# Layer 0's triangular inverses: one DMA for each matrix stack and each result, GpSimd in program order

## The chip, the cores and the metric

The kernel runs on one core of a Trainium2 chip. The metric is the device time of one execution in microseconds, median of several runs; inputs and weights lie in HBM at the start, all outputs in HBM at the end.

## The reference

One inference step of a two-layer streaming encoder: 512 prompt tokens and 32 sample tokens with a stored state, model width 1024, all in float32. Layer 0 is RWKV-7 time mixing with 24 heads of 64, layer 1 differential attention; both add a memory cross-attention of four heads and a SiLU gate, and a final RMSNorm ends the trunk. What matters here is layer 0's recurrence, which the reference writes as a scan over tokens:

```python
def step(S, inp):
    r_t, k_t, v_t, w_t, kk_t, a_t = inp
    sa = jnp.einsum('bhvk,bhk->bhv', S, -kk_t)
    S = (S * w_t[:, :, None, :] + sa[..., None] * (kk_t * a_t)[:, :, None, :]
         + v_t[..., None] * k_t[:, :, None, :])
    return S, jnp.einsum('bhvk,bhk->bhv', S, r_t)
```

## The kernel before, in words

Tokens lie along the free dimension and features on the partitions. The 24 heads are worked on two at a time: 12 pairs of heads, numbered 0 to 11, each 128 columns wide. The scan is done in chunks of 64 tokens. Within a chunk, the effect of the tokens on each other is a unit triangular matrix that has to be inverted; the kernel inverts its 32 x 32 diagonal blocks and merges two blocks into one of 64 afterwards. A pair has 34 such blocks (32 of the prompt, 2 of the sample).

The life of one pair p, by the functions that follow:

- `rw_prep` makes the decayed keys and queries, and with matmuls the chunk matrices `at` (and `ats` for the sample). It is a generator of 33 parts. Part 24 makes the product `rkk` (on GpSimd for pairs 3 to 11, on VectorE for pairs 0 to 2), part 26 writes the 34 blocks to a DRAM tile `sc1` (`sc<-at`, `sc<-ats` in the profile), and part 27 has the matmul `ps_q` that reads `rkk`. Part 2 starts the `up` loads of the next pair.
- `rw_invert` loads the blocks back, one block per partition (`m<-sc`; for pair 1 the tile is a borrowed gate buffer, `sg<-sc`), and inverts all at once on GpSimd: a copy of the identity (`u<-ui`), then 31 steps of a multiply (`tm<-u,m`, L861) and an add (`u<-u,tm`, L863). To use more partitions, the 32 rows of an inverse are dealt to NCL = 3 partitions, so every block is loaded three times: 102 partitions. The 32 prompt blocks stand on partitions 0 to 95 and the two sample blocks on 96 to 101; six DMAs load them (three of 32 rows and three of 2 rows, each row 4 KB).
- `rw_back` writes the results to DRAM (`sc<-u`), also with six DMAs, in pieces of 128 B.
- `rw_at` reads them from there into `at` and `ats` (`at<-sc`, `ats<-sc`, five DMAs).
- `rw_merge` merges the blocks; it begins with VectorE transposes `t1b<-at`, which TensorE's `ps_w` reads.
- `rw_values`, `rw_chain`, `rw_sample`, `rw_outputs`, `rw_finish` run the recurrence over the chunks, store the states (`out<-so`) and normalise (`ps_y`, `yt`).

Layer 0's loop is a hand-made software pipeline. A stage is the chain of one pair, 23 steps long (`go("chain", pr)`). The list PLAN says, for each of the 23 steps and each of its two halves, which parts of the other pairs are emitted there: `("inv", 2, 0, 0)` at entry 12, second half, means that the inverse of pair pr + 2 is emitted there (below: entry 12.5). The last two numbers are estimated times by which `next(main)` spreads the projection matmuls (`ps_g`) between the entries; zeros leave that spread alone. Before stage 0, the lists FILL0 to FILL3 do the same for the first pairs. `rsq` emits the reciprocal square roots on VectorE for the next pair's norms ("the roots").

The order is fixed on four queues: `Queue` ties each instruction of TensorE, VectorE, ScalarE and of SyncE, which issues nearly all DMAs, to the one emitted before it. So SyncE's DMA queue (SPq) issues strictly in the order of emission, and a DMA that waits holds up those behind it. GpSimd isn't tied: its instructions are called on `nc.gpsimd` and placed by the scheduler.

The constant `ui`, the identity dealt to the 102 partitions, is made from a column `cls` that holds the class 0, 1 or 2 of a partition; with the order above it takes nine small VectorE operations.

Of the kernel before, what the change touches and what calls it, by code (L numbers as in the profile page):

```python
# [9 lines left out]
F32 = mybir.dt.float32  # L10
# [4 lines left out]
ALU = mybir.AluOpType  # L15
# [40 lines left out]
    [[("prep", 2, 0, 1.1), ("smp", 0, 0.21, 0.29)], [("prep", 2, 0, 0.86)]],  # L56
    [[("prep", 2, 1.1, 1.37)], []],
    [[("smp", 0, 0.21, 0)], [("prep", 2, 0, 0.9)]],
    [[("prep", 2, 1.1, 1.37)], [("back", 1, 0, 0)]],
    [[("smp", 0, 0.6, 0.85)], []],  # L60
    [[("prep", 2, 0.5, 0.58)], [("at", 1, 0, 0), ("fin", -1, 0, 1.0)]],
    [[("prep", 2, 0.36, 0.43)], [("inv", 2, 0, 0), ("fin", -1, 0, 0.84)]],
    [[("prep", 2, 0.36, 0.43)], [("fin", -1, 0, 0), ("prep", 3, 0, 0)]],
    [[("prep", 2, 0.25, 0)], [("fin", -1, 0, 0.98)]],
    [[("prep", 2, 0.4, 0), ("smp", 0, 0.11, 0)], [("prep", 3, 0, 0.6)]],
    [[("prep", 3, 0.53, 0)], [("mrg", 1, 0, 0.86)]],
    [[("prep", 3, 0.11, 0.17), ("mrg", 1, 0.9, 0)], [("rsq", 0, 0, 1.5)]],
    [[("prep", 3, 0.33, 0)], [("fin", -1, 0, 0.88)]],
    [[("prep", 3, 0.33, 0)], [("prep", 3, 0, 0.1), ("fin", -1, 0.6, 1.0)]],
# [4 lines left out]
SHIFTED, KEPT = 13, 24  # L74
LAM = 5
EARLY = 5
SPLIT = {10: (18,), 11: (1, 5, 9, 13)}
MPLAN = {10: [(0, 0), (2, 0), (3, 0), (4, 0), (5, 0), (6, 0), (6.5, 1), (7, 0), (8, 0), (9, 0), (10, 0), (11, 0), (11.5, 0), (12.5, 1),
# [12 lines left out]
NCL = 3  # L91
NBLK = 34
# [16 lines left out]
class Trunk:  # L109
# [77 lines left out]
    def consts_rwkv(self, c):  # L187

        nc, a = self.nc, self.a
# [40 lines left out]
        cl = c.tile([NCL * NBLK, 1], F32, name="cl")  # L230
        nc.gpsimd.iota(cl[:], pattern=[[0, 1]], base=0, channel_multiplier=1, allow_small_or_imprecise_dtypes=True)
        cls = c.tile([NCL * NBLK, 1], F32, name="cls")
        self.ve.tensor_scalar(cls[:], cl[:], 32.0, None, ALU.is_ge)
        for at, w in ((64, 1.0), (96, -2.0), (98, 1.0), (100, 1.0)):
            cl2 = c.tile([NCL * NBLK, 1], F32, name=f"cl{at}")
            self.ve.tensor_scalar(cl2[:], cl[:], float(at), None, ALU.is_ge)
            self.ve.scalar_tensor_tensor(cls[:], cl2[:], w, cls[:], ALU.mult, ALU.add)
        nc.gpsimd.iota(ii[:], pattern=[[NCL, nr], [-1, 32]], base=0, channel_multiplier=0,
                       allow_small_or_imprecise_dtypes=True)
        self.ve.tensor_scalar(self.ui[:], ii[:], cls[:, 0:1], 0.0, ALU.add, ALU.is_equal)  # L240
# [398 lines left out]
    def rw_prep(self, st, rkv):  # L639
# [108 lines left out]
        decayed(zr, 1, nk, de, 0)  # L748
        yield
        k2 = k  # L750
        spare = nc.gpsimd if pr > 2 else self.ve
        self.ve.tensor_tensor(k2[:], k[:], kf[:], ALU.mult)
        yield
        ba = p.tile([P, T], F32, tag="ta", name="ba", bufs=1)
# [85 lines left out]

    def rw_invert(self, st):

        nc, p, sc1 = self.nc, self.rb, st["sc1"]
# [12 lines left out]
        tm = p.tile([NCL * NBLK, self.nr, 32], F32, tag="tm", name="tm", bufs=1)  # L856
        for kx in range(31):
            n = kx // NCL + 1
            wd = 31 - kx
            sh = [NCL * NBLK, n, wd]  # L860
            nc.gpsimd.tensor_tensor(tm[:, :n, :wd], u3[:, :n, kx : kx + 1].to_broadcast(sh),  # L861
                                    m3[:, kx : kx + 1, kx + 1 :].to_broadcast(sh), ALU.mult)
            nc.gpsimd.tensor_tensor(u3[:, :n, kx + 1 :], u3[:, :n, kx + 1 :], tm[:, :n, :wd], ALU.add)  # L863

    def rw_back(self, st):

        u3 = st["u3"]
        st["sc2"] = [self.dp.tile([m, 32, 32], F32, tag=f"sc2{m}", name=f"sc2{m}", bufs=2) for m in (32, 2)]
        for o, t in zip((0, 96), st["sc2"]):
            m = t.shape[0]  # L870
            for q in range(NCL):
                n = len(range(q, 32, NCL))
                self.se.dma_start(t[:, q : 32 : NCL, :], u3[o + q * m : o + q * m + m, :n, :])

    def rw_at(self, st):

        at, ats, sc2 = st["at"], st["ats"], st["sc2"]
# [556 lines left out]
    def layer0(self, mem):  # L1434
# [6 lines left out]
        with ExitStack() as ctx:  # L1441
# [16 lines left out]
            for q in (1, 0, 2):  # L1458
# [1 line left out]
            sts = [{"pr": pr} for pr in range(NPAIR)]  # L1460
            run, mit = {}, {}
            make = {"fin": self.rw_finish, "val": self.rw_values, "mrg": self.rw_merge, "smp": self.rw_sample,
                    "out": self.rw_outputs, "chain": self.rw_chain}

            def go(kind, pr):

                if kind == "rsq":
                    self.rsqrt(self.r20[:], self.q20[:], self.rk0, "nt")
                elif 0 <= pr < NPAIR:
                    if kind in ("inv", "back", "at"):  # L1470
                        {"inv": self.rw_invert, "back": self.rw_back, "at": self.rw_at}[kind](sts[pr])
# [92 lines left out]
            def fill(n, each=6):  # L1564

                while n > 0:
                    for _ in range(min(n, each)):
                        next(main)
                    n -= each
                    self.some(LATER)  # L1570

            self.ordered = True
            for k, n in enumerate(FILL0):
                go("prep", 0)
                if k == 3:
# [18 lines left out]
            for k, n in enumerate(FILL2):  # L1594
                go("prep", 2)
                if k == 3:
                    go("rsq", 2)
                    go("inv", 1)
                    go("back", 0)
                    go("at", 0)  # L1600
                fill(n)
# [562 lines left out]
    def run(self):  # L2164
# [72 lines left out]
```

## Time and profile before

| | |
|---|---|
| median of 3 runs | 1403.37 us (1402.63 to 1403.77) |
| the profiled execution | 1402.28 us, span 1400.5 us |
| TensorE (PE) busy | 1361.5 us, 97% |
| VectorE (DVE) busy | 934.6 us, 67% |
| ScalarE (ACT) busy | 828.6 us, 59% |
| GpSimd (POOL) busy | 371.7 us, 27% |
| mean granted TensorE clock | 0.996 |

The span is the profiler's account of the execution from its first to its last instruction; the execution's own time has 1.8 us around it. Layer 0 takes the first half, up to about 700 us. In a row of a timeline stand the start and the duration in us, the engine, the line, the operation, the tiles as out<-in, the shape, the count of merged instructions, and in brackets the idle time before and what ended it. Most instructions carry L106, the line of the helper that records them, so they are told apart by their tiles. A row of waits reads: who waited for whom, us in total, times, longest. A row of a window reads: the stretch, its length, then the busy time and count of PE, PEld (weight loads), DVE, ACT and POOL, then the granted clock, the share of the 16 DMA engines and GB/s (where the row is of one engine alone, only that engine's time stands there).

### The profile page before, as it was taken

How to read it: one execution, taken by the hardware profiler on the slowest of the kernel's cores; microseconds unless marked ns; L12 is line 12 of the kernel's file. 1: busy time of each engine (PE TensorE's matmuls, PEld its weight loads, DVE VectorE, ACT ScalarE, POOL GpSimd, SP SyncE). 2: the span in 40 equal slices, each digit the busy share in tenths (PEclk: the TensorE clock that was granted, in tenths of full speed). 3: DMA queues.
4: the chain of work that ended last, by engine and by line, in shares of the span. 5: the costliest groups of instructions: out<-in, count | busy, mean ns of one | idle time of the engine just before them, and what ended most of it. 6: DMA issues, size and time to landing. Idle time of an engine off the chain costs nothing.

```text
span 1400.5 us, 31939 instructions
## 1 busy us (share of the span) xinstructions
PE 1361.5 (97%) x11893; PEld 1296.7 (93%) x11893; DVE 934.6 (67%) x2345; ACT 828.6 (59%) x2304; POOL 371.7 (27%) x841
## 2 busy tenths in 40 slices
PE   8999999999999999999999999999999999999997
PEld 6988899999998998897899999999999999999997
DVE  5765777787877787676753476676467756767443
ACT  5756677767776777565543366664466546665222
POOL 2136567555865576520000040000000001001000
PEclk9999999999999999999999999999999999999999
DMA  7543222332233222342474473333333322332321
GB/s 224 155 118 80 49 57 76 84 96 62 67 82 99 61 77 73 87 131 64 121 206 118 120 218 108 92 92 93 101 92 94 104 73 84 97 106 84 91 76 72
DMA packets 264036, 139.45 MB, mean 100 GB/s; under 512 B 57721, under 2 KB 252802, under 8 KB 263882
## 3 DMA queue, kind: packets, MB, share of 16 engines
q1 hardware_dynamic: 263818, 137.41, 34.9%
q8 instruction: 94, 1.54, 0.5%
q14 instruction: 60, 0.49, 0.1%
q10 hardware_dynamic: 64, 0.02, 0.0%
HBM read 111.12 MB, written 22.91 MB: 96 GB/s over the span
## 4 chain that ended last, share of the span: by engine, by line
PE 81%; DVE 8%; ACT 3%; issue 2%; POOL 2%; DMA 2%; SPq 1%; DVEq 0%; ACTq 0%; POOLq 0%
PE ps_g L106 57%; PE ps_c L106 4%; PE ps_s L106 2%; PE ps_o L106 2%; PE ps_at L106 2%; DVE wlo L106 1%; PE ps_v L106 1%; SPq L106 1%; PE ps_mm L106 1%; PE ps_mo L106 1%; POOL tm L861 1%; PE ps_aT L106 1%; PE ps_yc L106 1%; POOL u L863 1%; PE ps_kv L106 1%
## 5 line engine op out<-in xcount | busy, mean ns | idle before, releaser
L106 PE MATMUL ps_g<-hh,whi 128*128 128x272 f32 x1808 | 541.0, 300 | 0.4 <-DVE memk L106 0.2
L106 PE MATMUL ps_g<-hh,wlo 128*128 128x272 f32 x1808 | 536.0, 297 | 1.6 <-DVE wlo L106 1.6
L106 PE MATMUL ps_g<-hl,whi 128*128 128x272 f32 x1808 | 532.1, 295 | 0.6 <-DVE hl L106 0.3
L106 PEld LDWEIGHTS ps_g<-hh,wlo 128*128 128x128 f32 x1808 | 341.7, 189 | 6.3 <-DVE wlo L106 2.3
L106 PEld LDWEIGHTS ps_g<-hh,whi 128*128 128x128 f32 x1808 | 341.9, 189 | 5.8 <-DVE og L106 0.6
L106 PEld LDWEIGHTS ps_g<-hl,whi 128*128 128x128 f32 x1808 | 341.8, 189 | 4.6 <-DVE hl L106 1.3
L106 DVE TENSOR_TENSOR wlo<-raw,whi 128x512 fp32r<-128x512 f32 x314 | 220.9, 714 | 123.0 <-ACT whi L106 119.2
L106 ACT CAST whi<-raw 128x512 fp32r<-128x512 f32 x314 | 189.1, 619 | 109.5 <-PE ps_g L106 61.4
L861 POOL TENSOR_TENSOR tm<-u,m 102x84 f32<-102x84 f32 (+23 forms) x341 | 143.7, 421 | 165.5 <-DMA m<-sc 139.7
L863 POOL TENSOR_TENSOR u<-u,tm 102x84 f32<-102x84 f32 (+23 forms) x341 | 148.3, 435 | 26.6
L106 PE MATMUL ps_g<-hi,whi 128*128 128x272 f32 x512 | 148.9, 291 | 0.0
L106 PE MATMUL ps_g<-hi,wlo 128*128 128x272 f32 x512 | 147.5, 288 | 0.5 <-DVE wlo L106 0.5
L106 PE MATMUL ps_g<-lo,whi 128*128 128x272 f32 x512 | 147.4, 288 | 0.0
L1333 POOL TENSOR_TENSOR lo<-og,hi 128x544 fp32r<-128x544 f32 x8 | 13.2, 1652 | 359.7 <-ACT hi L106 359.2
L106 PEld LDWEIGHTS ps_g<-hi,wlo 128*128 128x128 f32 x512 | 96.4, 188 | 0.8 <-DVE wlo L106 0.7
L106 PEld LDWEIGHTS ps_g<-hi,whi 128*128 128x128 f32 x512 | 96.4, 188 | 0.0
L106 PEld LDWEIGHTS ps_g<-lo,whi 128*128 128x128 f32 x512 | 96.4, 188 | 0.0
L106 ACT ACTIVATE pt<-ps_s,snm 128x128 f32<-128x128 f32 (+3 forms) x96 | 51.0, 532 | 41.7 <-DVE snm L106 41.6
L106 DVE SCALAR_TENSOR_TENSOR SB<-ps_c,dl,sd 64x64 f32<-64x64 f32 x168 | 47.4, 282 | 40.9 <-PE ps_c L106 37.7
L1754 POOL TENSOR_TENSOR hl<-hn,hh 128x544 fp32r<-128x544 f32 x8 | 12.5, 1567 | 211.3 <-ACT hh L106 211.2
L106 ACT ACTIVATE sg<-ps_g 128x272 f32<-128x272 f32 x64 | 25.3, 396 | 57.6 <-PE ps_g L106 53.0
L106 ACT COPY sv<-ps_c 64x64 f32<-64x64 f32 x192 | 39.5, 206 | 33.3 <-PE ps_c L106 31.2
(402 smaller groups left out, 2578.3 us busy)
## 6 DMA issues: line engine op xcount, KB each, us to landing
raw<-in_rw_in_dram SPq DMA_DIRECT2D x114, 256.0 KB
raw<-in_df_in_dram SPq DMA_DIRECT2D x112, 256.0 KB
raw<-in_w_out_dram SPq DMA_DIRECT2D x64, 256.0 KB
oscr<-sg SPq DMA_DIRECT2D x16, 272.0 KB
lo<-oscr SPq DMA_DIRECT2D x16, 272.0 KB
m<-sc SPq DMA_DIRECT2D x33, 128.0 KB
raw<-in_w_mem_v_dram SPq DMA_DIRECT2D x16, 256.0 KB
kh<-kh SPq DMA_DIRECT2D x24, 136.0 KB
```

Of the source, the lines that this page charges most:

```text
L106: return lambda *a, **k: self.trunk.tie(self, issue(*a, **k))
L861: nc.gpsimd.tensor_tensor(tm[:, :n, :wd], u3[:, :n, kx : kx + 1].to_broadcast(sh), m3[:, kx : kx + 1, kx + 1 :].to_broadcast(sh), ALU.mult)
L863: nc.gpsimd.tensor_tensor(u3[:, :n, kx + 1 :], u3[:, :n, kx + 1 :], tm[:, :n, :wd], ALU.add)
L1333: (self.nc.gpsimd if g % 2 and self.o1 else self.ve).tensor_tensor(lo[:], t, hi[:].bitcast(F32), ALU.subtract)
L1754: nc.gpsimd.tensor_tensor(self.hl[:, k, :], h[:], self.hh[:, k, :].bitcast(F32), ALU.subtract)
```

## The change

- The blocks stand on the partitions in the order q x 34 + block, so a single DMA loads all 102 rows, with the source repeated three times by a broadcast dimension, and a single DMA writes all results, to a DRAM tile with a row more per block. `rw_at` reads from that tile. `cls` takes three VectorE operations.
- A fifth queue ties GpSimd's instructions: the inverse and `rkk` are emitted on `self.ge`.
- `rw_invert` becomes a generator with two parts: the load, the copy and the first 22 of the 31 steps, and the last 9 steps (HALFWAY = 21).
- PLAN: the inverse of pair pr + 2 moves from entry 12.5 to entry 16.5 (first part), with the second part at entry 7 of the next stage; `back` moves from 9.5 to 10.5, `at` from 11.5 to 12.0. In FILL0 and FILL2 both parts are emitted together.

```diff
-    [[("prep", 2, 1.1, 1.37)], []],                                   # entry 7
+    [[("prep", 2, 1.1, 1.37), ("inv", 1, 0, 0)], []],
...
-    [[("prep", 2, 1.1, 1.37)], [("back", 1, 0, 0)]],                  # entries 9 to 12
-    [[("smp", 0, 0.6, 0.85)], []],
-    [[("prep", 2, 0.5, 0.58)], [("at", 1, 0, 0), ("fin", -1, 0, 1.0)]],
-    [[("prep", 2, 0.36, 0.43)], [("inv", 2, 0, 0), ("fin", -1, 0, 0.84)]],
+    [[("prep", 2, 1.1, 1.37)], []],
+    [[("smp", 0, 0.6, 0.85)], [("back", 1, 0, 0)]],
+    [[("prep", 2, 0.5, 0.58)], [("fin", -1, 0, 1.0)]],
+    [[("at", 1, 0, 0), ("prep", 2, 0.36, 0.43)], [("fin", -1, 0, 0.84)]],
...
-    [[("prep", 3, 0.53, 0)], [("mrg", 1, 0, 0.86)]],                  # entry 16
+    [[("prep", 3, 0.53, 0)], [("mrg", 1, 0, 0.86), ("inv", 2, 0, 0)]],
...
+HALFWAY = 21
...
-        self.ve.tensor_scalar(cls[:], cl[:], 32.0, None, ALU.is_ge)
-        for at, w in ((64, 1.0), (96, -2.0), (98, 1.0), (100, 1.0)):
-            cl2 = c.tile([NCL * NBLK, 1], F32, name=f"cl{at}")
-            self.ve.tensor_scalar(cl2[:], cl[:], float(at), None, ALU.is_ge)
-            self.ve.scalar_tensor_tensor(cls[:], cl2[:], w, cls[:], ALU.mult, ALU.add)
+        self.ve.tensor_scalar(cls[:], cl[:], float(NBLK), None, ALU.is_ge)
+        self.ve.tensor_scalar(cl[:], cl[:], float(2 * NBLK), None, ALU.is_ge)
+        self.ve.tensor_tensor(cls[:], cls[:], cl[:], ALU.add)
...
-        spare = nc.gpsimd if pr > 2 else self.ve
+        spare = self.ge if pr > 2 else self.ve
...
     def rw_invert(self, st):
+        yield
...
-        for q in range(NCL):
-            self.se.dma_start(m3[q * 32 : q * 32 + 32], sc1[:32])
-            self.se.dma_start(m3[96 + 2 * q : 98 + 2 * q], sc1[32:])
-        nc.gpsimd.tensor_copy(u3, self.ui[:])
+        self.se.dma_start(m3, sc1[:].unsqueeze(0).to_broadcast([NCL, NBLK, 32, 32]))
+        self.ge.tensor_copy(u3, self.ui[:])
...
-            nc.gpsimd.tensor_tensor(tm[:, :n, :wd], ...)
-            nc.gpsimd.tensor_tensor(u3[:, :n, kx + 1 :], ...)
+            self.ge.tensor_tensor(tm[:, :n, :wd], ...)
+            self.ge.tensor_tensor(u3[:, :n, kx + 1 :], ...)
+            if kx == HALFWAY:
+                yield
 
     def rw_back(self, st):
         u3 = st["u3"]
-        st["sc2"] = [self.dp.tile([m, 32, 32], F32, tag=f"sc2{m}", name=f"sc2{m}", bufs=2) for m in (32, 2)]
-        for o, t in zip((0, 96), st["sc2"]):
-            m = t.shape[0]
-            for q in range(NCL):
-                n = len(range(q, 32, NCL))
-                self.se.dma_start(t[:, q : 32 : NCL, :], u3[o + q * m : o + q * m + m, :n, :])
+        st["sc2"] = sc2 = self.dp.tile([NBLK, self.nr, NCL, 32], F32, tag="sc2", name="sc2", bufs=2)
+        self.se.dma_start(sc2[:].rearrange("b n q t -> q b n t"), u3)
 
     def rw_at(self, st):
-                                  sc2[0][n : n + 8].rearrange("b s t -> s b t"))
-        self.se.dma_start(ats[64:96, 1, :, :32], sc2[1].rearrange("h s t -> s h t"))
+                                  sc2[n : n + 8, :32].rearrange("b s t -> s b t"))
+        self.se.dma_start(ats[64:96, 1, :, :32], sc2[32:, :32].rearrange("h s t -> s h t"))
...
                 if k == 26:                       # FILL0; the same for ("inv", 1) in FILL2
                     go("inv", 0)
+                    go("inv", 0)
...
-        self.te, self.ve, self.ae, self.se = (Queue(self, e) for e in (nc.tensor, nc.vector, nc.scalar, nc.sync))
+        self.te, self.ve, self.ae, self.se, self.ge = (
+            Queue(self, e) for e in (nc.tensor, nc.vector, nc.scalar, nc.sync, nc.gpsimd))
```

More of the change, by code (lines that the diff above doesn't have):

```diff
@@ L841, in rw_invert @@
     def rw_invert(self, st):
-        nc, p, sc1 = self.nc, self.rb, st["sc1"]
+        yield
+        p, sc1 = self.rb, st["sc1"]
         if st["pr"] == 1:
@@ L860, in rw_invert @@
             sh = [NCL * NBLK, n, wd]
-            nc.gpsimd.tensor_tensor(tm[:, :n, :wd], u3[:, :n, kx : kx + 1].to_broadcast(sh),
+            self.ge.tensor_tensor(tm[:, :n, :wd], u3[:, :n, kx : kx + 1].to_broadcast(sh),
                                     m3[:, kx : kx + 1, kx + 1 :].to_broadcast(sh), ALU.mult)
-            nc.gpsimd.tensor_tensor(u3[:, :n, kx + 1 :], u3[:, :n, kx + 1 :], tm[:, :n, :wd], ALU.add)
+            self.ge.tensor_tensor(u3[:, :n, kx + 1 :], u3[:, :n, kx + 1 :], tm[:, :n, :wd], ALU.add)
+            if kx == HALFWAY:
+                yield
     def rw_back(self, st):
         u3 = st["u3"]
-        st["sc2"] = [self.dp.tile([m, 32, 32], F32, tag=f"sc2{m}", name=f"sc2{m}", bufs=2) for m in (32, 2)]
-        for o, t in zip((0, 96), st["sc2"]):
-            m = t.shape[0]
-            for q in range(NCL):
-                n = len(range(q, 32, NCL))
-                self.se.dma_start(t[:, q : 32 : NCL, :], u3[o + q * m : o + q * m + m, :n, :])
+        st["sc2"] = sc2 = self.dp.tile([NBLK, self.nr, NCL, 32], F32, tag="sc2", name="sc2", bufs=2)
+        self.se.dma_start(sc2[:].rearrange("b n q t -> q b n t"), u3)
     def rw_at(self, st):
-        at, ats, sc2 = st["at"], st["ats"], st["sc2"]
+        at, ats, sc2 = st["at"], st["ats"], st["sc2"].rearrange("b n q t -> b (n q) t")
         for e in range(2):
@@ L1462, in layer0 @@
             make = {"fin": self.rw_finish, "val": self.rw_values, "mrg": self.rw_merge, "smp": self.rw_sample,
-                    "out": self.rw_outputs, "chain": self.rw_chain}
+                    "out": self.rw_outputs, "chain": self.rw_chain, "inv": self.rw_invert}
             def go(kind, pr):
@@ L1469, in go @@
                 elif 0 <= pr < NPAIR:
-                    if kind in ("inv", "back", "at"):
-                        {"inv": self.rw_invert, "back": self.rw_back, "at": self.rw_at}[kind](sts[pr])
+                    if kind in ("back", "at"):
+                        {"back": self.rw_back, "at": self.rw_at}[kind](sts[pr])
                         return
@@ L1597, in layer0 @@
                     go("rsq", 2)
+                    go("inv", 1)
                     go("inv", 1)
```

## The prediction

> **What bounds the kernel now.** The page comes first, then the waits of each engine, then the timelines of one stage.
>
> ```profile
> span 1400.5 us, 31939 instructions
> PE 1361.5 (97%) x11893; PEld 1296.7 (93%) x11893; DVE 934.6 (67%) x2345; ACT 828.6 (59%) x2304; POOL 371.7 (27%) x841
> ```
>
> TensorE leaves 39 us of the span, so a gain in layer 0 can only be small, while any wait put in front of TensorE costs its full length. Which waits it has, and which GpSimd (POOL) and the DMA queue (SPq) have:
>
> ```profile
> PE ps_y L106 <- DVE yt L106: 5.0, 10, 0.9
> ...
> PE ps_q L106 <- POOL rkk L781: 0.3, 1, 0.3
> ```
>
> ```profile
> POOL tm L861 <- DMA m<-sc: 139.7, 11, 43.6
> ```
>
> ```profile
> SPq L106 <- POOL u L863: 77.4, 10, 10.4
> ```
>
> TensorE waits once, for 0.3 us, on something that stands behind an inverse (`rkk`). GpSimd waits 139.7 us for matrices, and the DMA queue 77.4 us in ten stages for an inverse to end: inverses and SPq take turns in a loop. One turn of it in GpSimd's timeline, between the inverses of pairs 6 and 7 (the first row is the last step of inverse 6):
>
> ```profile
> 382.17 0.23 POOL L863 TENSOR_TENSOR u<-u,tm 102x11 f32<-102x11 f32 x1
> ...
> 395.95 0.24 POOL L861 TENSOR_TENSOR tm<-u,m 102x31 f32<-102x31 f32 x1 [9.46 <-DMA m<-sc]
> ...
> 427.72 0.23 POOL L863 TENSOR_TENSOR u<-u,tm 102x11 f32<-102x11 f32 x1
> 427.91 1.34 POOL L781 TENSOR_TENSOR rkk<-rkv 128x544 f32<-128x544 f32 x1
> ```
>
> SPq's timeline in that gap, in program order:
>
> ```profile
> 382.43 2.36 SPq L106 DMA_DIRECT2D sc<-u  x6
> 385.20 0.94 SPq L106 DMA_DIRECT2D raw<-in_rw_in_dram  x2
> 386.24 1.92 SPq L106 DMA_DIRECT2D sc<-at  x4
> ...
> 388.76 1.85 SPq L106 DMA_DIRECT2D at<-sc  x4
> ...
> 391.20 2.47 SPq L106 DMA_DIRECT2D m<-sc  x6
> 394.43 0.36 SPq L106 DMA_DIRECT2D out_dram<-so  x1
> 394.89 1.11 SPq L106 DMA_DIRECT2D up<-in_rw_w_up_dram  x2
> 396.06 1.23 SPq L106 DMA_DIRECT2D up<-in_rw_a_up_dram  x2
> ```
>
> And the two places where TensorE and VectorE set the pace of a stage: `ps_q`, TensorE's first reader of `rkk` (entry 12 of PLAN), and `t1b`, the start of the merge (second half of entry 16):
>
> ```profile
> 385.92 0.62 PE L106 MATMUL ps_q<-rkk,hb 128*128 128x272 f32 x2
> ```
>
> ```profile
> 394.80 0.89 DVE L106 STREAM_TRANSPOSE t1b<-at 32x256 f32<-32x256 f32 x2
> ```
>
> ```profile
> 431.79 0.62 PE L106 MATMUL ps_q<-rkk,hb 128*128 128x272 f32 x2
> ```
>
> A stage is 431.79 - 385.92 = 45.87 us. `rkk` ends at 429.25 and is read at 431.79: the slack of the whole chain is 2.5 us.
>
> **The change part by part.** Place of the matrices' load: it goes from entry 12.5 to entry 16.5, behind `t1b`. In SPq's order it thereby passes behind `out<-so` (entry 15, which waits for the state that TensorE turns there) and the four `up` loads (entry 15.5). These end at 396.06 + 1.23 = 397.29, so the issue moves from 391.20 to 397.3: 6.1 us later, 2.5 us after `t1b`. Nothing on SPq can pull it forward; the readiness of `so`, not the queue, holds the row at 394.43 (SPq was free from 393.67).
>
> One DMA for six: issuing falls from 2.47 us to about 0.41 (a sixth). On SPq that is off TensorE's path. Today the first step starts 395.95 - 393.67 = 2.28 us after the last issue. What a single 408 KB load (102 rows of 4 KB) adds to this isn't in the trace; it depends on over how many of the 16 DMA engines it is spread. The trace shows that it differs, in three short stretches (last columns: DMA share of 16 engines, GB/s): during `sc<-u` of 32 rows, during `sc<-u` of 2 rows, and during `m<-sc` of 32 rows of 4 KB.
>
> ```profile
> 383.30:383.60 0.30, 0.30 (x5) 0.30 (x4) 0.30 (x2) 0.06 (x1) 0.30 (x1) 1.00 0.82 125
> 384.95:385.09 0.14, 0.14 (x4) 0.14 (x3) 0.13 (x1) 0.00 (x0) 0.00 (x0) 1.00 0.12 19
> 392.48:392.70 0.22, 0.22 (x3) 0.22 (x4) 0.21 (x2) 0.21 (x2) 0.00 (x0) 1.00 0.92 372
> ```
>
> Two rows keep 0.12 x 16 = 2 engines busy, 32 rows all of them: a DMA is divided by its outermost dimension. The new load's outermost dimension in DRAM is the threefold repeat, the new store's (`q b n t`) also three, against 102 partitions in SBUF. Three is the only count near that divides both, so I estimate three engines. One engine moves 372/(0.92 x 16) = 25.3 GB/s in 4 KB rows, so 417.8 KB take 5.5 us on three; on sixteen 417.8/372 = 1.1 us. From issue to first step: 0.41 + 2.28 + 5.5 = 8.2 us, or 3.8 us. These are the two ends; I take 8.2, because the two-row stretch is the nearest row for a small outer count. The store in 128 B pieces moves 19/2 = 9.5 GB/s per engine: 143.6 KB (102 x 11 x 128 B) take 5.0 us on three.
>
> The Trainium skill's page "DMA: Bandwidth & Descriptors" (section "Rules for kernel authors") says the same of this form by name: a leading zero-stride broadcast of c copies confines the whole DMA to at most c engines. By that rule the sum is the one with 8.2 us, and the stretch with 0.12 agrees with it for two rows; no run yet shows it for three. The same section also speaks for the change, since it tells one to coalesce many small transfers into a large one; by that alone the sum would be the one with 3.8 us.
>
> GpSimd's order: `rkk` of pair p (entry 8.5) is queued behind the second part of inverse p - 1 (entry 7), the first part behind the load. In the timeline above `rkk` stands behind the inverse already, so the order and the split change nothing on GpSimd; the later start does. Behind `rkk` waits `ps_q`, behind that TensorE with everything.
>
> The loop after the change, pair by pair: `ps_q` to the next `t1b` 440.66 - 431.79 = 8.87;
>
> ```profile
> 440.66 0.89 DVE L106 STREAM_TRANSPOSE t1b<-at 32x256 f32<-32x256 f32 x2
> ```
>
> to the issue 2.5; to the first step 8.2; the inverse; `rkk` and its reader 1.4. An inverse takes 32.0 us, and 27.0 in the last pair, beside less other work:
>
> ```profile
> 395.95:427.95 32.00, 27.22 (x63) 1.00 0.23 66
> 577.10:604.13 27.03, 22.22 (x62) 1.00 0.39 117
> ```
>
> TensorE would stand still for some 7 of the 32 us, which I price at the faster rate: 32.0 - 7 x 5/32 = 30.9. Lastly a stop of TensorE has a tail in the granted clock:
>
> ```profile
> 549.00:552.00 3.00, 1.49 (x13) 1.28 (x12) 2.84 (x6) 2.64 (x8) 2.63 (x5) 1.00 0.00 0
> 552.00:556.00 4.00, 4.00 (x23) 4.00 (x22) 3.91 (x9) 3.13 (x8) 3.53 (x7) 0.57 0.00 0
> ```
>
> After 1.5 us of idle time the clock is 0.57 over 4 us, which costs 1.7 us. Loop: 8.87 + 2.5 + 8.2 + 30.9 + 1.4 + 1.7 = 53.6 us against 45.87 now.
>
> Nine stages read a `rkk` of GpSimd (pairs 3 to 11):
>
> ```profile
> 202.78 0.73 PE L106 MATMUL ps_q<-rkk,hb 128*128 128x272 f32 x2 [0.34 <-POOL rkk L781]
> ```
>
> ```profile
> 567.92 0.62 PE L106 MATMUL ps_q<-rkk,hb 128*128 128x272 f32 x2
> ```
>
> First: inverse 2 is loaded at 167.8 (its `t1b`) + 2.5 = 170.3, starts at 178.5, ends about 30.4 us later as now (170.96 to 201.4), and `ps_q` comes at 210.3: 7.5 late. Then eight loops: 8 x 53.6 - (567.92 - 202.78) = 63.7. With the last clock tail 1.7: +72.9 us.
>
> Start of layer 0: load 1, store 0 and the return of inverse 0 follow each other on SPq, and `t1b` of pair 0 already waits for them:
>
> ```profile
> 125.58 2.61 SPq L106 DMA_DIRECT2D sg<-sc  x6
> 128.29 2.34 SPq L106 DMA_DIRECT2D sc<-u  x6
> 130.90 1.78 SPq L106 DMA_DIRECT2D at<-sc  x4
> ```
>
> ```profile
> 133.50 0.43 DVE L106 STREAM_TRANSPOSE t1b<-at 32x256 f32<-32x256 f32 x1 [0.53 <-DMA at<-sc]
> ```
>
> On the same three engines load and store run after each other: 125.58 + 0.41 + 2.28 + 5.5 + 5.0 = 138.8 before `at<-sc` may go, against 130.90: +7.9, with the clock's tail +9 (on sixteen engines 0, or 2 us won, as SPq is free earlier). In later stages the store lands 0.05 + 0.41 + 2.28 + 5.0 = 7.7 us after the inverse's end, `at<-sc` takes 2.4 (388.76 to 391.20) and lands 2.3 later: 12.4 us, against 1.4 + 8.87 + 1.7 = 12.0 until `t1b`. That is level and costed at nothing, as the matrices' load stands behind both; there is no slack, and each us over it would make the merge wait.
>
> Other edits: six of nine one-column VectorE operations go (0.15 us each, at 42 to 44 us, GpSimd waiting for a matrix until long after): 0. Roots and `ps_y`: GpSimd now starts behind the roots; that can win at most the 5.0 us of the waits above, and I take 2.
>
> Sum against the profiled execution's own 1402.28 us: + 72.9 + 9 - 2 = 1482; the median of the runs, 1403.37, stands 1.1 above that. I take 4 off, half a microsecond a loop: in the 2.5 us behind `t1b` SPq waits for ScalarE's copy of the state (row at 394.43), and ScalarE has less queued after a stop. Prediction: 1478.
>
> **The rivals.** (a) All sixteen engines: the loop is 53.6 - 4.4 = 49.2 us, the first `ps_q` 3.1 late, the rest 8 x 49.2 - 365.1 = 28.5, tail 1.7, start 0: +33 - 2, about 1434. For it: the present loads use all engines; against it: the two-row stretch. (b) Faster: the inverse fits. It needs issue to last step within 45.87 - 8.87 - 2.5 - 1.4 = 33.1 us, so on sixteen engines an inverse of under 29.3 us, which the last pair's 27.0 shows to be possible where little runs beside it; every full stage had 32. Then `ps_y`'s 5.0 us go at best: 1398 to 1401. (c) It does nothing: inverse just fits, gains lost to load: 1403.
>
> **How the numbers follow.** Within 0.2% (2.8 us) is about what a measurement of this kernel cannot tell from no change. Three engines 0.65 (its own range 1455 to 1495: the tail and the faster inverse left out or doubled), (a) 0.21 (1412 to 1450), (b) 0.08, (c) 0.06. Slower 0.86. The range is the first case and most of (a): 1415 to 1495.
>
> **What would show it.** TensorE's waits should have `ps_q <- rkk` as the first row, nine times 5 to 8 us; the load should land some 8 us after its issue, with a DMA share near 0.19 (3 of 16); the clock should dip after each stop; `ps_w <- t1b` of pair 0 should wait about 8 us. A load that lands within 4 us makes it (a); an inverse under 29 us makes it (b). It is wrong in whole if `rkk` starts before the inverse's second part.

## The result, and the profile after

The changed kernel takes 1495.95 us (median of 4 runs, 1494.77 to 1498.32) against 1403.04 us (1402.63 to 1403.77) for the kernel before: a ratio of 1.0664, 95% interval 1.0645 to 1.0682. It is slower, as forecast, but by 92.9 us where 75 were forecast. The profiled execution took 1495.89 us, its span is 1494.2 us and its mean granted clock 0.969 (0.996 before).

In this kernel the helpers that record an operation carry L107, GpSimd's too, so rows are told apart by engine and tiles. The head of the page and its chain of the work that ended last:

```profile
span 1494.2 us, 31763 instructions
PE 1383.9 (93%) x11893; PEld 1318.5 (88%) x11893; DVE 935.1 (63%) x2339; ACT 828.0 (55%) x2304; POOL 355.8 (24%) x841
...
PE 71%; POOL 8%; DMA 6%; DVE 5%; SPq 4%; issue 3%; ACT 3%; DVEq 0%; POOLq 0%; ACTq 0%
```

The span grew by 93.7 us. TensorE is busy 22.4 us longer with the same 11893 matmuls (1383.9 against 1361.5), and stands still 110.3 us instead of 39.0. TensorE was 81% of the chain before and is 71% now; POOL, DMA and SPq, the loop of the inverses, have 18% of it instead of 5%. The waits of TensorE, then of GpSimd, then of the DMA queue:

```profile
PE ps_w L107 <- DVE t1b L107: 73.4, 22, 7.6
PE ps_q L107 <- POOL rkk L107: 4.2, 4, 1.6
```

```profile
POOL tm L107 <- DMA m<-sc: 219.2, 11, 48.4
...
POOL u L107 <- DMA sc<-u: 60.4, 9, 7.0
```

```profile
SPq L107 <- POOL u L107: 192.1, 11, 20.9
```

In the kernel before, the rows of the merge and of the copy of the identity were:

```profile
PE ps_w L106 <- DVE t1b L106: 2.5, 5, 1.1
```

```profile
POOL u L855 <- DMA sc<-u: 20.1, 9, 2.3
```

TensorE's new wait is at the start of the merge (`ps_w`, which needs `t1b`, which needs `at<-sc`), 22 times with 73.4 us in all, against 2.5 us. GpSimd waits 219.2 us for matrices (139.7 before), and SPq 192.1 us for an inverse to end (77.4 before; with the one inverse whose tile is called `u3r` in the program, 194.0 against 98.5): both sides of the loop wait longer for each other, which is how a loop looks that nothing else covers. The row `u <- sc<-u` has grown from 20.1 to 60.4 us: the next inverse's copy of the identity waits until the result has left its tile; the load is later still, so it costs nothing.

One turn of the loop, first on SPq, from the load of inverse 7 to that of inverse 8:

```profile
455.69 0.77 SPq L107 DMA_DIRECT2D m<-sc  x1
...
497.71 0.76 SPq L107 DMA_DIRECT2D sc<-u  x1
498.56 4.29 SPq L107 DMA_DIRECT2D raw<-in_rw_in_dram  x2
502.94 1.94 SPq L107 DMA_DIRECT2D sc<-at  x4
504.99 0.41 SPq L107 DMA_DIRECT2D sc<-ats  x1
505.49 1.85 SPq L107 DMA_DIRECT2D at<-sc  x4
507.44 0.40 SPq L107 DMA_DIRECT2D ats<-sc  x1
507.93 0.38 SPq L107 DMA_DIRECT2D out_dram<-so  x1
508.40 1.14 SPq L107 DMA_DIRECT2D up<-in_rw_w_up_dram  x2
509.59 1.23 SPq L107 DMA_DIRECT2D up<-in_rw_a_up_dram  x2
510.86 1.14 SPq L107 DMA_DIRECT2D raw<-in_rw_in_dram  x2
512.05 0.77 SPq L107 DMA_DIRECT2D m<-sc  x1
```

and on GpSimd (first step, `rkk`, last step) and TensorE:

```profile
466.11 0.24 POOL L107 TENSOR_TENSOR tm<-u,m 102x31 f32<-102x31 f32 x1 [17.61 <-DMA m<-sc]
...
488.81 1.33 POOL L107 TENSOR_TENSOR rkk<-rkv 128x544 f32<-128x544 f32 x1
...
497.46 0.23 POOL L107 TENSOR_TENSOR u<-u,tm 102x11 f32<-102x11 f32 x1
```

```profile
507.73 0.31 PE L107 MATMUL ps_w<-t1b,at 32*32 32x32 f32 x2 [7.07 <-DVE t1b L107]
```

Three things are to be seen. From the end of the inverse (497.69) to the next load's issue (512.05) SPq works off its list with hardly a gap; the loop runs through SPq. The load is issued at 455.69 and its reader starts at 466.11, 10.4 us later. And `rkk` stands between the two parts of the inverse, not behind it, which is not what the prediction said (below).

How many DMA engines the two new DMAs use, in two stretches of the load and one of the store (last three columns: granted clock, DMA share of 16 engines, GB/s):

```profile
457.90:459.00 1.10, 1.10 (x12) 1.10 (x11) 1.04 (x4) 1.07 (x3) 0.00 (x0) 1.00 0.20 45
459.00:461.00 2.00, 2.00 (x44) 1.81 (x42) 1.99 (x5) 0.97 (x4) 0.00 (x0) 1.00 0.18 66
498.90:500.00 1.10, 1.10 (x14) 1.09 (x9) 0.35 (x2) 1.10 (x4) 0.00 (x0) 1.00 0.17 26
```

Shares of 0.17 to 0.20 are 2.7 to 3.2 of 16 engines, for both. And the clock around TensorE's stop of 7.07 us:

```profile
506.00:508.00 2.00, 0.28 (x2) 0.18 (x2) 0.44 (x1) 0.00 (x0) 0.00 (x0) 0.50 0.34 52
508.00:512.00 4.00, 3.26 (x41) 3.16 (x41) 3.37 (x13) 1.60 (x5) 0.00 (x0) 0.50 0.23 51
512.00:516.00 4.00, 4.00 (x27) 4.00 (x27) 1.90 (x5) 2.92 (x9) 0.00 (x0) 0.75 0.57 168
```

It is granted at half for 4 us after the work has resumed, and still at 0.75 in the next four: the same matmuls take longer, and so TensorE is busier. In the turn above SPq goes through its list with hardly a gap, so these 22.4 us tell how TensorE spends the added time and are no term of the loop.

### The profile page after: what moved, and what is told of

Read it like the earlier page. It is cut to its first block, busy times and chain, and to the rows that moved or that the text cites. A ratio compares the mean times of both kernels' runs of the same rounds, so it can differ in the third digit from the quotient of the medians.

```text
span 1494.2 us, 31763 instructions
## 1 busy us (share of the span) xinstructions
PE 1383.9 (93%) x11893; PEld 1318.5 (88%) x11893; DVE 935.1 (63%) x2339; ACT 828.0 (55%) x2304; POOL 355.8 (24%) x841
## 4 chain that ended last, share of the span: by engine, by line
PE 71%; POOL 8%; DMA 6%; DVE 5%; SPq 4%; issue 3%; ACT 3%; DVEq 0%; POOLq 0%; ACTq 0%
PE ps_g L107 51%; SPq L107 4%; POOL u L107 4%; POOL tm L107 4%; DMA m<-sc 3%; PE ps_c L107 3%; PE ps_s L107 2%; PE ps_o L107 2%; DMA at<-sc 1%; DMA sc<-u 1%; PE ps_mm L107 1%; PE ps_at L107 1%; PE ps_mo L107 1%; DVE wlo L107 1%; PE ps_v L107 1%
## 5 line engine op out<-in xcount | busy, mean ns | idle before, releaser
L107 PE MATMUL ps_g<-hh,whi 128*128 128x272 f32 x1808 | 547.2, 303 | 0.4 <-DVE memk L107 0.2
L107 PE MATMUL ps_g<-hh,wlo 128*128 128x272 f32 x1808 | 541.1, 300 | 1.4 <-DVE wlo L107 1.4
L107 PE MATMUL ps_g<-hl,whi 128*128 128x272 f32 x1808 | 537.4, 298 | 0.6 <-DVE hl L107 0.3
L107 PEld LDWEIGHTS ps_g<-hh,whi 128*128 128x128 f32 x1808 | 347.7, 193 | 6.0 <-DVE og L107 0.6
L107 PEld LDWEIGHTS ps_g<-hh,wlo 128*128 128x128 f32 x1808 | 347.0, 192 | 5.9 <-DVE wlo L107 1.8
L107 PEld LDWEIGHTS ps_g<-hl,whi 128*128 128x128 f32 x1808 | 347.4, 192 | 4.6 <-DVE hl L107 1.2
L107 DVE TENSOR_TENSOR wlo<-raw,whi 128x512 fp32r<-128x512 f32 x314 | 222.7, 720 | 124.8 <-ACT whi L107 116.3
L107 ACT CAST whi<-raw 128x512 fp32r<-128x512 f32 x314 | 189.0, 619 | 108.8 <-PE ps_g L107 61.0
L107 POOL TENSOR_TENSOR tm<-u,m 102x84 f32<-102x84 f32 (+23 forms) x341 | 139.7, 410 | 244.2 <-DMA m<-sc 219.2
L107 PE MATMUL ps_g<-hi,whi 128*128 128x272 f32 x512 | 148.7, 290 | 0.0
L107 PE MATMUL ps_g<-hi,wlo 128*128 128x272 f32 x512 | 147.7, 288 | 0.5 <-DVE wlo L107 0.5
L107 PE MATMUL ps_g<-lo,whi 128*128 128x272 f32 x512 | 147.4, 288 | 0.0
L107 POOL TENSOR_TENSOR u<-u,tm 102x84 f32<-102x84 f32 (+23 forms) x341 | 138.0, 405 | 26.6
L1329 POOL TENSOR_TENSOR lo<-og,hi 128x544 fp32r<-128x544 f32 x8 | 13.2, 1651 | 359.6 <-ACT hi L107 359.1
L107 PEld LDWEIGHTS ps_g<-hi,wlo 128*128 128x128 f32 x512 | 96.3, 188 | 0.7 <-DVE wlo L107 0.7
L107 PEld LDWEIGHTS ps_g<-hi,whi 128*128 128x128 f32 x512 | 96.5, 188 | 0.0
L107 PEld LDWEIGHTS ps_g<-lo,whi 128*128 128x128 f32 x512 | 96.4, 188 | 0.0
L107 PE MATMUL ps_w<-t1b,at 32*32 32x32 f32 x384 | 15.7, 233 | 73.4 <-DVE t1b L107 73.4
L107 DVE SCALAR_TENSOR_TENSOR SB<-ps_c,dl,sd 64x64 f32<-64x64 f32 x168 | 47.5, 283 | 57.1 <-PE ps_c L107 50.8
L107 PEld LDWEIGHTS ps_w<-t1b,at 32*32 32x32 f32 x384 | 12.7, 144 | 77.6 <-DVE t1b L107 69.7
L107 ACT ACTIVATE pt<-ps_s,snm 128x128 f32<-128x128 f32 (+3 forms) x96 | 50.9, 531 | 41.8 <-DVE snm L107 41.6
L107 ACT COPY sv<-ps_c 64x64 f32<-64x64 f32 x192 | 39.3, 205 | 40.5 <-PE ps_c L107 38.5
```

The source lines that it names most:

```text
L107: return lambda *a, **k: self.trunk.tie(self, issue(*a, **k))
L1329: (self.nc.gpsimd if g % 2 and self.o1 else self.ve).tensor_tensor(lo[:], t, hi[:].bitcast(F32), ALU.subtract)
```

## The experiments

The theory after the two traces, A: SPq, GpSimd and the return form a loop that was 45.4 us long before (from the issue of `at<-sc` 2.68 to the load's, then 4.46 + 32.00 + 6.26 of the table below) and so just hidden under TensorE's 45.87 us a stage; three separate lengthenings of it add up and count in full: the load's place behind `out<-so`, `up` and `raw`, the load on three engines, and a return that is late behind the store. The rival, B: the new ties of GpSimd, the cut around `rkk` or the clock cost the most, and undoing a DMA gives little back.

The parts of a turn, in us, means over pairs 4 to 9, taken from the starts and ends that the rows above show for one pair. "wait" is from `t1b` of the pair before to the load's issue; "load" from its issue to the first step; "inverse" from the first step to the last; "return" from the last step to the issue of `at<-sc`; "t1b" from there to `t1b`. Their sum is the turn. In "before" and "early, whole" TensorE sets the turn, not the loop, and a load issued ahead of `t1b` has a negative wait.

| kernel | median us | ratio, 95% | wait | load | inverse | return | t1b | turn |
|---|---|---|---|---|---|---|---|---|
| before | 1403 | 1 | -2.95 | 4.46 | 32.00 | 6.26 | 6.11 | 45.87 |
| after | 1495.95 | 1.0645 to 1.0682 | 5.12 | 9.66 | 31.48 | 7.86 | 1.81 | 55.93 |
| load and store in rows | 1461.81 | 1.0407 to 1.0438 | 5.13 | 5.49 | 32.32 | 7.76 | 2.12 | 52.83 |
| load alone in rows | 1465.78 | 1.0426 to 1.0461 | 5.00 | 5.41 | 32.35 | 7.98 | 2.03 | 52.78 |
| three loads of 34 rows | 1530.09 | 1.0887 to 1.0922 | 5.14 | 12.31 | 31.39 | 7.95 | 1.83 | 58.62 |
| two loads on 16 engines, before's stores by step 3 | 1458.66 | 1.0379 to 1.0413 | 5.09 | 5.15 | 32.28 | 7.60 | 2.11 | 52.23 |
| before's transfers, after's order | 1441.31 | 1.0259 to 1.0304 | 5.00 | 5.43 | 31.64 | 6.26 | 1.99 | 50.32 |
| after, first part early | 1465.26 | 1.0431 to 1.0462 | 0.58 | 9.77 | 32.35 | 8.02 | 1.86 | 52.59 |
| rows, first part early | 1422.58 | 1.0123 to 1.0153 | 0.62 | 4.88 | 32.53 | 7.72 | 2.04 | 47.78 |
| before's transfers, first part early | 1411.13 | 1.0044 to 1.0083 | 0.27 | 4.78 | 32.67 | 6.35 | 2.24 | 46.32 |
| the same, uncut ("early, whole") | 1402.90 | 0.9992 to 1.0010 | -2.59 | 4.67 | 31.78 | 6.28 | 5.70 | 45.84 |
| after, uncut | 1493.28 | 1.0626 to 1.0658 | 4.28 | 10.06 | 29.12 | 7.77 | 4.56 | 55.79 |

**Load and store in rows.** After's layout and order, but both transfers as six DMAs again, 32 or 2 rows each:

```diff
-        self.se.dma_start(m3, sc1[:].unsqueeze(0).to_broadcast([NCL, NBLK, 32, 32]))
+        for q in range(NCL):
+            self.se.dma_start(m3[q * NBLK : q * NBLK + 32], sc1[:32])
+            self.se.dma_start(m3[q * NBLK + 32 : q * NBLK + NBLK], sc1[32:])
...
-        self.se.dma_start(sc2[:].rearrange("b n q t -> q b n t"), u3)
+        for q in range(NCL):
+            o = q * NBLK
+            self.se.dma_start(sc2[:32, :, q, :], u3[o : o + 32])
+            self.se.dma_start(sc2[32:, :, q, :], u3[o + 32 : o + NBLK])
```

> The changed kernel with load and store each cut into six DMAs again (three of 32 rows, three of 2), at the changed places. Theory A (an SPq loop, each part adds): in the changed kernel one turn is 56.3 us = 4.7 from t1b to the load's issue + 10.4 to the first step + 31.6 of GpSimd + 7.8 to at<-sc + 1.7 to t1b. Six DMAs give back 10.4 - 4.75 = 5.7 on the load and 7.8 - 6.1 = 1.7 on the return: 48.9 us, against a stage of 45.87, so about 9 x 3.0 = 27 us over the kernel before: 1425 to 1435 us. Rival B (the form of the DMAs alone): 1403. Rival C (the places alone): 1490.

Measured 1461.81 us, 27 us over the upper end of what was expected. The load's part falls from 9.66 to 5.49 us and 34 us come back, 10.6 of them at the start (`t1b` of pair 2 comes 5.3 us later than in the kernel before, not 15.9). But the turn is 52.83 us, not 48.9. The return stays at 7.76 where 6.1 was expected: the theory had the single store's share of it too large, and the next run says why. The rest of the miss is the load (5.49 for 4.75), the wait (5.13 for 4.7), the way to `t1b` (2.12 for 1.7) and the inverse, which takes 32.32 us here and 31.48 in after.

**Load alone in rows.** The first half of that edit, with the single store kept.

> The changed kernel with only the load cut into six DMAs. Theory A: 56.3 - 5.7 = 50.6 us a turn, 9 x 4.7 = 43 us and about 4 of the start: 1445 to 1455 us. If the engines under the load are not the cause, the time stays at 1495.

Measured 1465.78 us, where 1445 to 1455 was expected, and 4 us (0.3%) over the run above, with the same turn (52.78 and 52.83). The 4 us lie in the start (`t1b` of pair 2 comes 8.9 us later than before, and 5.3 in the run above); in a turn the single store costs no more than six stores of that form. Both delay `at<-sc`, in two different ways. With the single store its issue is short and the next DMAs' is long:

```profile
476.30 0.77 SPq L107 DMA_DIRECT2D sc<-u  x1
477.17 4.28 SPq L107 DMA_DIRECT2D raw<-in_rw_in_dram  x2
```

With six stores in rows (here from the kernel with the first part early) the stores themselves take the time:

```profile
442.12 3.99 SPq L107 DMA_DIRECT2D sc<-u  x6
446.22 0.93 SPq L107 DMA_DIRECT2D raw<-in_rw_in_dram  x2
```

and with before's six stores, in after's order, neither does:

```profile
456.38 2.36 SPq L107 DMA_DIRECT2D sc<-u  x6
458.83 0.94 SPq L107 DMA_DIRECT2D raw<-in_rw_in_dram  x2
```

The two rows end 5.15, 5.03 and 3.39 us after the first one's start. The 0.77 us of a single store are thus no gain: the queue is held for 3.3 us more at the DMAs behind it (4.28 us against 0.94).

**Before's transfers in after's order.** Before's layout, loads and stores; after's PLAN, tie and cut. What is left of the change's lengthenings is the load's place.

```diff
-        self.se.dma_start(m3, sc1[:].unsqueeze(0).to_broadcast([NCL, NBLK, 32, 32]))
+        for q in range(NCL):
+            self.se.dma_start(m3[q * 32 : q * 32 + 32], sc1[:32])
+            self.se.dma_start(m3[96 + 2 * q : 98 + 2 * q], sc1[32:])
...
-        self.se.dma_start(sc2[:].rearrange("b n q t -> q b n t"), u3)
+        for o, t in zip((0, 96), st["sc2"]):
+            m = t.shape[0]
+            for q in range(NCL):
+                n = len(range(q, 32, NCL))
+                self.se.dma_start(t[:, q : 32 : NCL, :], u3[o + q * m : o + q * m + m, :n, :])
```

> The changed order, the GpSimd tie and the split stay; layout, loads and stores are those of before (six and six DMAs, [11,32] form). What is left of the change is the place of the load. Theory A (place of load, load on three engines and a return held up behind the single store, added up along SP's loop): a turn of 7.0 (at<-sc to load issue) + 4.5 to 5.4 (issue to first step) + 32.2 (steps) + 6.3 (last step to at<-sc, as before) = 50.0 to 50.9 us, so 9 stages of +4.1 to +5.0 over before's 45.87, and a start stall of 4 to 8: 1440 to 1455. Last step to at<-sc 6.3, not the 7.8 of the single store. Theory B (the two DMAs cost little, the tie of GpSimd and its order against the roots cost the most): at or above the 1462 of the kernel with both transfers in rows.

Measured 1441.31 us, a turn of 50.32, a return of 6.26: theory A, in all three numbers. Only the start, priced at 4 to 8 us there, cost nothing (`t1b` of pair 2 comes 1.4 us later than before). Against 1402.9 us the place, with the cut around `rkk`, costs 38 us, and the change of the transfers another 55.

**Two loads over sixteen engines.** Before's stores (the partitions taken by a step of 3) and the load as two DMAs with the blocks outermost, so that row 3b + q holds block b for class q (`cls` is the partition number modulo 3, five VectorE operations at the start):

```diff
+        self.se.dma_start(m3[:96], sc1[:32].unsqueeze(1).to_broadcast([32, NCL, 32, 32]))
+        self.se.dma_start(m3[96:], sc1[32:].unsqueeze(1).to_broadcast([2, NCL, 32, 32]))
...
+                self.se.dma_start(t[:, q : 32 : NCL, :], u3[o + q : o + NCL * m : NCL, :n, :])
```

> The order of after, before's six stores; the load is two DMAs with the 32 block rows outermost (96 and 6 partitions, row 3b+q), so 16 engines serve it with two issues. Theory A: the single load's cost is its three engines, not its single issue: issue to first step 3.9 to 5.0 us against 9.7, turn 49 to 50.5, 1433 to 1450, no more than 5 us off the kernel with before's loads in this order. Rival (a broadcast load of three copies in one DMA is slow however it is spread): issue to first step 8 or more, 1475 to 1490.

Measured 1458.66 us: a miss in the total, but the load answers the question. Its part is 5.15 us, a little less than six DMAs need (5.41 to 5.49) and a little over the 3.9 to 5.0 expected, with the same broadcast and the same bytes as the single load's 9.66:

```profile
484.04 1.33 SPq L107 DMA_DIRECT2D m<-sc  x2
...
468.75 3.89 SPq L107 DMA_DIRECT2D sc<-u  x6
```

```profile
487.00:488.00 1.00, 1.00 (x11) 1.00 (x10) 0.92 (x3) 0.76 (x2) 0.00 (x0) 1.00 0.68 204
```

In this stretch nearly all the traffic is the load's rows of 4 KB, and 0.68 is 11 engines on the average. In the traces' packets the 102 rows of 4 KB take 2.8 us here (486.0 to 488.8) and 7.7 us with the single load (457.7 to 465.4). So the broadcast isn't what is slow, it is the three engines; that the single issue isn't the cause either, the next run shows. The miss lies mostly in the store, which I had not thought changed: by a step of 3 its issue takes 3.89 us, not 2.36, and the return is 7.60, not 6.26. That is 1.3 of the 1.9 us by which the turn is longer than with before's transfers; another 0.6 is the inverse (32.28 against 31.64).

**Three loads of 34 rows.** Only the load is changed:

```diff
-        self.se.dma_start(m3, sc1[:].unsqueeze(0).to_broadcast([NCL, NBLK, 32, 32]))
+        for q in range(NCL):
+            self.se.dma_start(m3[q * NBLK : q * NBLK + NBLK], sc1[:])
```

> Only the load is changed: three DMAs of 34 rows in place of one of 3 x 34. Theory A (the number of engines that a transfer is spread over follows the count of its outermost rows: 3 gave three engines, 32 gave sixteen; 34 has no divisor under 17 but 2): each load takes two engines, DMA share near 0.12 while it runs, and issue to first step is 12 us or more if the three take the same two engines: 1515 to 1540, slower than the single load. Rival (three separate transfers overlap, the cost was one queue entry being served alone): issue to first step under 7, 1455 to 1475.

Measured 1530.09 us, slower than the single load; 12.31 us from issue to first step. With more DMAs the transfer is slower, which of the two explanations on record only the count of the rows fits. While the load runs with little beside it:

```profile
478.00:480.00 2.00, 2.00 (x45) 1.69 (x44) 2.00 (x5) 1.27 (x4) 0.00 (x0) 1.00 0.13 53
```

A share of 0.13 is two engines. The Trainium skill, page "DMA: Bandwidth & Descriptors", section "Why a DMA increments its semaphore by 16 and not by 1", has a DMA spread over the largest number up to 16 that divides the outermost dimension of both its sides. The runs agree: 3 repeats against 102 rows gave 0.18 (three engines), 34 against 34 gave 0.13 (two), 32 against 32 gave 0.92 in the kernel before (the prediction's stretch), and 32 against 96 gave 0.68 above, which excludes two or three engines without showing all sixteen.

**The first part early.** After, with the load and first part back at entry 12.5, behind `at`:

```diff
-    [[("at", 1, 0, 0), ("prep", 2, 0.36, 0.43)], [("fin", -1, 0, 0.84)]],
+    [[("at", 1, 0, 0), ("prep", 2, 0.36, 0.43)], [("inv", 2, 0, 0), ("fin", -1, 0, 0.84)]],
...
-    [[("prep", 3, 0.53, 0)], [("mrg", 1, 0, 0.86), ("inv", 2, 0, 0)]],
+    [[("prep", 3, 0.53, 0)], [("mrg", 1, 0, 0.86)]],
```

> The changed kernel with the inverse's first part emitted at entry 12.5 again, directly behind the return, with the single DMAs. Theory A: the load no longer passes behind out<-so, up and raw, so from at<-sc to the load's issue it takes 2.4 us in place of 6.55: a turn of 56.3 - 4.1 = 52.2 us, 9 x 6.3 = 57 us and the 8 us at the start over the kernel before: 1460 to 1472 us. Rival B (form of the DMAs alone): as the changed kernel, 1495. Rival C (places alone): 1403.

Measured 1465.26 us, as theory A had it: the wait goes from 5.12 to 0.58 us, 31 us come back.

**Rows and the first part early.** Both edits at once.

> Load and store as six DMAs in rows, and the inverse's first part at 12.5 behind `at`: both terms undone together. Theory A: they add, and so do what undoing each gave (34.1 and 30.7 us): a turn of about 2.5 + 5.4 + 32.3 + 7.7 = 47.9 us, 1419 to 1435. Theory B (one hidden wait, such as the clock's tail after each stop or rkk between the parts, limits both): 1450 or more.

Measured 1422.58 us with a turn of 47.78 us (47.9 expected). Undone singly, the two gave 34.1 and 30.7 us; together they give 73.4, so neither hides the other. This is what theory B excluded. They don't simply add, either: in each of the three runs the inverse takes 0.8 to 1.1 us longer than in after (32.32, 32.35 and 32.53 against 31.48), which is paid twice in the two single runs and once here.

**Uncut.** After, with HALFWAY = 31: all steps stand in the first part, and `rkk` stands behind the whole inverse.

> The changed kernel with the inverse emitted whole at entry 16.5, so that rkk stands behind all 31 steps in place of between the parts. By the prediction's working (which had rkk behind the inverse) the loop through rkk and ps_q is 4.7 + 10.4 + 30.3 + 1.4 + 8.9 = 55.7 us, with the clock's tail 57.4, and becomes the longer one: 1495 to 1505 us with ps_q <- rkk as TensorE's first wait. By theory A alone (through the return) a turn is shorter by rkk's 1.35 us, 54.9: 1483 us with ps_w <- t1b as the first wait.

Measured 1493.28 us, 2.7 us (0.2%) under after: the cut brings nothing there. The time lies just under the first of the two expectations, and the first wait is the one that it named; the wait only changes its name:

```profile
PE ps_q L107 <- POOL rkk L107: 66.2, 9, 8.9
PE ps_w L107 <- DVE t1b L107: 9.6, 6, 7.0
```

A turn through `rkk` in this kernel is as long as one through the return in after (55.79 and 55.93 us).

**The tie and the cut alone.** Before's transfers, the first part at 12.5; once cut as in after, once uncut.

> The transfers of before (six loads, six stores, its layout) and the inverse's first part at entry 12.5; what is left of the change is GpSimd's tie, the cut into two parts around rkk, and the later places of `back` and `at`. Theory A (the three terms were the load's place, its three engines and the return behind the single store): the turn measured with loads and stores in rows at this place, 47.8 us, less 1.6 us that before's store saves in issuing = 46.2, which is level with the 45.87 that TensorE needs: 1402 to 1410. Rival (the tie or the cut costs something of its own): 1415 or more. If the roots and ps_y gain what TensorE waited for there (5.0 us in all), 1397 to 1401.

> As the one with before's transfers and the first part at 12.5, but all 31 steps in the first part (rkk behind the whole inverse, as in before). Theory A: the inverse ends about 2 us earlier after its start (29.1 + nothing of rkk inside against 31 to 32) but rkk comes behind it, as before with 2.2 us to spare: 1402 to 1408, within 3 us of the cut one. Rival (the cut is what kept ps_q from waiting): 1410 or more, with ps_q waiting for rkk.

Measured 1411.13 us cut (its six runs are 1407.2 to 1408.2 or 1414.1 to 1414.5; the profiled one took 1408.16) and 1402.90 us uncut, ratio 1.0001. The expectations were right in part. The cut kernel is 1 us over its range, though its turn, 46.32, is near the 46.2 expected. The tie of GpSimd, the roots and the later `back` and `at` cost and bring nothing (the uncut one), as theory A had it, but the two were to be within 3 us of each other and lie 8 apart. The rival's number for the uncut one (1410 or more, with `ps_q` waiting) didn't come. The waits of TensorE, cut and then uncut:

```profile
PE ps_w L107 <- DVE t1b L107: 6.0, 11, 1.3
```

```profile
PE ps_y L107 <- DVE yt L107: 4.4, 10, 0.6
```

With `rkk`'s 1.35 us inside it the inverse ends 0.9 us later (32.67 against 31.78), and the loop of 46.32 us is half a microsecond longer than TensorE's stage. Uncut it is hidden again.

Read upwards from 1402.90 us, the change is made of steps that were each run: the cut +8.2 (4.6 or 11.3 by its two groups of runs), the six stores in after's layout and form +11.5 (1422.58), the load and store as one DMA each +42.7 (1465.26), and the load's place +30.7 (1495.95). No version here beats the kernel before; TensorE's 45.87 us a stage lie under all of them.

## Why the prediction was right or wrong

**Right.** The sign and the mechanism: a loop through SPq, GpSimd and the return that no longer fits into a stage. Three engines for both DMAs (0.19 forecast, 0.18 to 0.20 and 0.17 measured), and the rival of sixteen is out. The start: `t1b` of pair 0 was to wait some 8 us; from the issue of load 1 to `at<-sc` it takes 12.8 us, for 13.2 forecast, and TensorE's wait is

```profile
138.09 0.28 PE L107 MATMUL ps_w<-t1b,at 32*32 32x32 f32 x2 [7.56 <-DVE t1b L107]
```

That the two loops, through `rkk` and through the return, are near level was right as well: in the uncut kernel the one through the return has only the 0.5 to 2.2 us to spare by which `out<-so` waits for `so` behind it.

**Right by luck.** The return was forecast at 7.7 us from the inverse's end to `at<-sc`, and is 7.86, but it is made in another way. The forecast had `at<-sc` wait until the store has landed. GpSimd's copy waits for just that, and it starts 6.65 us after the inverse's end (497.69):

```profile
504.34 0.48 POOL L107 CAST u<-ui 102x352 f32<-102x352 bf16 x1 [6.65 <-DMA sc<-u]
```

`at<-sc` is issued 1.15 us later, at once behind `sc<-ats`: the two `raw` loads that take 4.29 us to issue set its time, and the forecast left them out of this term. The sum up to the loop agrees by luck too: the start and the first late inverse were to make 9 + 7.5 = 16.5 us, and `t1b` of pair 2 comes 15.9 later than before, but that of pair 0 5.0 later (load 1 is issued at 122.86, 2.7 us earlier than before) and that of pair 1 7.2, and the first late inverse adds 8.7.

**Wrong, the order.** The prediction and the text above it, with its diff, put the second part at entry 7. In PLAN it stands in the first half of entry 9, behind `rkk` at 8.5. So `rkk` lies between the two parts, the first row of TensorE's waits is `ps_w <- t1b` and not `ps_q <- rkk`, and by the prediction's own last sentence it was wrong in whole there. It isn't what made the size wrong: the uncut kernel has the order that the prediction assumed, its first wait is the row forecast (nine times, up to 8.9 us), and it takes 1493.28 us, still 15 us over the forecast.

**Wrong, the sizes.** Over that kernel the terms of the loop can be held against the forecast one by one: `t1b` to the issue 4.28 us, not 2.5; issue to first step 10.06, not 8.2; the inverse 29.12, not 30.9; the rest (7.77 + 4.56) 12.33, not 1.4 + 8.87 + 1.7 = 11.97. In after, where the loop closes through the return, they are 5.12, 9.66, 31.48 with `rkk` inside, and 9.67. Either way the turn is 2.2 to 2.3 us longer than 53.6.

Two terms failed, the load's place and the load itself; in the uncut kernel an inverse forecast 1.8 us too long hides about half of that. The place was put at 2.5 us behind `t1b`, because the readiness of `so`, not the queue, was to set the time of `out<-so`, with only four `up` loads behind it. In the uncut kernel the first half of this is right (its `t1b` starts at 505.07):

```profile
502.94 0.40 SPq L107 DMA_DIRECT2D ats<-sc  x1
504.70 0.36 SPq L107 DMA_DIRECT2D out_dram<-so  x1
505.16 1.14 SPq L107 DMA_DIRECT2D up<-in_rw_w_up_dram  x2
506.35 2.12 SPq L107 DMA_DIRECT2D up<-in_rw_a_up_dram  x2
508.51 1.14 SPq L107 DMA_DIRECT2D raw<-in_rw_in_dram  x2
509.69 0.76 SPq L107 DMA_DIRECT2D m<-sc  x1
```

`out<-so` comes 1.4 us after `ats<-sc` has been issued and 0.37 us before `t1b`, as in the kernel before. What the forecast's list lacked are the two `raw` loads, 1.2 us; the remaining 0.6 us of the mean of 4.28 are single issues that took 1 us or more, as one of the `up` loads here. In after, the kernel that the forecast was about, the other half failed too: `t1b` comes 1.8 us behind `at<-sc`, SPq is later than `so`, and `out<-so` follows `ats<-sc` 0.09 us later in every turn. The queue sets its time, and four `up` loads and two `raw` loads go back to back behind it: 5.12 us. In the turn to pair 10, which has no `up` loads there, it is 2.08. The 4 us taken off, because SPq would wait for ScalarE's copy of the state, stood on the same reading, and nothing of it came.

The second term, the load, was priced from the transfer's rate in a short stretch and an issue of 0.41 us. The issue is 0.77 us, and at the 66 GB/s of the stretch from 459 to 461 us, where nothing else ran, 417.8 KB take 6.3 us, not 5.5 (9.66 - 0.77 - 2.28 leaves 6.6). From turn to turn the load's part is 8.5 to 10.4 us; what sets this wasn't tested.

The sum then comes out: the start and first inverse 15.9 for 16.5; the eight turns from pair 2 to pair 10 move `t1b` from 15.9 to 92.0 us late, 76.1 for 63.7 (a turn of 55.0 us on the average, as that to pair 10 takes 49.6); the end 1.7, which was forecast as a tail of the clock and agrees with it in the number alone, as `t1b` of pair 11 is 94.1 late; and the 4 and 2 us taken off did not come. That is 15.9 + 76.1 + 1.7 = 93.7, the difference of the spans (lateness is the start of a pair's `t1b` in one timeline less that in the other). The 2 us for `ps_y` are instructive: its waits did fall, from 5.0 to 0.7 us, but once SPq sets the stage, time won on TensorE is spent waiting at `ps_w`.

## What to carry to other kernels

Before a transfer is made into one DMA, look at the outermost count of both sides: it decides over how many engines the bytes go, and a broadcast of three copies put outermost made the load's part 4.2 us longer, though 1.7 us of issuing were saved. A loop of waits that is hidden by half a microsecond looks free in the profile, with waits of 0.3 us, but what is added to it beyond that counts in every stage, less what another part of the loop gains by it (here the inverse, by up to 1 us), and additions in different places nearly add up. When an instruction is moved on a queue that issues in order, count every row that it passes and ask how late the queue itself will be by then, not only when its neighbours were ready before.

## What the runs showed of the hardware that was not expected

- A DMA of many small pieces on few engines has a short issue of its own (0.76 us for the 102 x 11 pieces of 128 B) and holds up the queue's next issue: two `raw` loads took 4.29 us to issue behind it, 0.94 us behind six stores. Three engines alone don't do it: behind the load of pair 2, 102 pieces of 4 KB over three engines, two `raw` loads took 0.99 us (178.45). That a backlog of small pieces is the cause is not shown; no run varied their number.
- Six stores of pieces of 128 B took 2.36 us to issue in before's layout (blocks of 32 partitions), 3.99 us in after's layout, and 3.89 us with a partition step of 3. What sets this stays open.
- After each of the ten stops of 5.2 to 7.6 us the granted clock is 0.50 for the first 4 us of resumed work; TensorE's busy time grew by 22.4 us in this kernel.
